# New times for the first eight chunks of x and for the first forgetting head in a one-core transformer block

## The chip, the cores and the metric

The kernel runs on one core of one Trainium2 chip. The metric is the device time of one execution in microseconds (us); lower is better. Engines are named as in the profile: PE (matrix products), DVE (vector), ACT (scalar and activations), POOL, and SP, which here issues nearly all DMA transfers. Each engine works through its own instructions strictly in program order and waits where an operand or a buffer is not ready.

## What is computed

One residual block on x of 512 x 2048 numbers in float32: a norm, one combined projection, eight stick-breaking heads and eight forgetting heads, an output projection, and an MLP.

```python
h = rmsnorm(x, g_attn[l])
proj = jnp.einsum('bsd,de->bse', h, w_in[l])
...
# forgetting heads, for each block i of 128 rows
z = jnp.einsum('bhqd,bhkd->bhqk', qb, kb).astype(jnp.float32) * scale
z = z + c[:, :, i * Q_BLOCK:end, None] - c[:, :, None, :end]
p = jax.nn.softmax(jnp.where(causal, z, -jnp.inf), axis=-1)
outs.append(jnp.einsum('bhqk,bhkd->bhqd', p.astype(v.dtype), vb))
...
mixed = jnp.concatenate([head_rmsnorm(o_sb, g_out_sb[l]),
                         head_rmsnorm(o_fox, g_out_fox[l])], axis=-1)
x = x + jnp.einsum('bse,ed->bsd', mixed, w_out[l])
h2 = rmsnorm(x, g_mlp[l])
u = jax.nn.relu(jnp.einsum('bsd,df->bsf', h2, w_up[l]))
x = x + jnp.einsum('bsf,fd->bsd', u * u, w_down[l])
```

## The kernel before

**Three products for one.** A float32 operand is split in a high part (a rounded cast, on ACT) and a low part (the operand less its high part, on DVE). A product is then three PE products: high by high, high by low, low by high. `mm3` issues the three (L76 to L78), which is why most PE rows carry these lines whatever they belong to. Weights follow the same way: a DMA to `wraw`, ACT's cast to `wh` (L168), DVE's rest `wl` (L171). The tile names `accq` (projections of the attention), `s` (scores), `w` (softmax weights), `pt` (their transposes), `ph` and `pl` (high and low part of these), `vh` and `vl` (of the values), `o` (a head's output) and `ssq` (its sum of squares) appear in the rows of the trace. `uh` and `ul` are high and low part of queries and keys, made from `qf`.

**The order is a table of times.** The program does not issue work directly. It collects jobs with `plan.at(t, f, ...)`, where t is a time on an imagined clock, and `plan.run()` calls them in the order of t. What counts is only the order that results: a job's time says behind and ahead of which others its instructions come on each engine. SP's transfers are issued by such jobs too. Nothing else arranges the engines' instructions.

**Stage 1, 0 to about 38 us.** x comes in 16 chunks of 128 columns, and the first value columns of the projection are summed over them in the order `seq` = 0, 1, 8, 9, 2, 10, 3, 11, 4, 12 and so on; `mm_at[j]` is the time of chunk j, 1.93 apart. For each chunk PE turns four blocks into the tile `tr` (`turn_x`, L256), of which there are two; ACT makes the high part (`x_high`, L259), DVE the low part (`x_low`, L262), and both tiles are also read for a scaled copy that the sums of the projection use later: `x_more` (DVE, L265) for the chunks below 8, `x_sum` (DVE, L271) and `x_right` (ACT, L268) for the others. The weights are `wfirst`. Chunks 0, 1, 8 and 9 are multiplied by kind: `first_part` (L299) does the four blocks of rows with high by high, then with high by low, then with low by high, and a table `early` gives each of their jobs a time. All others use `first_values`, which goes block by block with `mm3`, and share one list of times. `square_x` (ACT, L275) sums squares for the norm.

**Attention.** A period of `TPER` = 27.05 handles one head: its projections run in pieces between the steps of other heads. For a forgetting head, `plan_fox` places: `load` (a copy `cb` of the summed log forget gates), `start` (DVE adds them to the scores, L823; POOL masks, L768), `maxed` (DVE, L830 and L831), `soft` (ACT's exponentials with sums, L835), `scale` (DVE, L838 and L840). Then come `turn` (PE, ten transposes, L850), `p_high` (ACT, L859), `p_low` (DVE, L862), the twelve products of `o`, `square` (ACT, L889 to L891), `square_low` (DVE, L894) and `norm_sums` (PE, L899 and L900). The first head of all, number 0 in the order, is a forgetting one, and its steps lie between 184 and 216 us of the trace. `low_v` (L758) makes the low part of the values that it uses.

**Work beside it.** `WeightSums` forms sums of blocks of the output weights on DVE (L937, `mixed<-mixed` in the rows), with high and low parts on the way (`tboth`, L929 and L932; `thi`, L941 and L945) and stores to DRAM. `whole(m, t)` places them for m = 0 to 3. `scale_u`, `high_u` and `low_u` (L726 to L736) take queries and keys out of `accq`.

Of the kernel before, what the change touches and what calls it, by code (L numbers as in the profile page):

```python
# [19 lines left out]
NH = 8  # L20
# [16 lines left out]
def block_kernel(ctx, tc, x, g_attn, w_in, b_f, g_out_sb, g_out_fox, w_out, g_mlp, w_up, w_down, g_final, y):  # L37
# [101 lines left out]
    K8 = KC // 2  # L139
# [72 lines left out]
    with ExitStack() as stage:  # L212
# [23 lines left out]
        plan = Plan()  # L236
# [43 lines left out]
        c0, m = v_columns(order[0]), 2 * P + NH  # L280
# [25 lines left out]
        seq = [0, 1, K8, K8 + 1] + [j for k in range(2, K8) for j in (k, k + K8)]  # L306
# [36 lines left out]
        for j in seq[:4]:  # L343
            for part, wait in zip(("hh", "hl", "lh"), (0.0, 0.6, 1.1)):
                plan.at(mm_at[j] + wait, first_part, j, *pieces[j], part)
# [13 lines left out]
        for k in range(2, K8):  # L359
            t, j = mm_at[k], k + K8  # L360
            for jj, dt in ((k, 0.0), (j, step)):
                for half in range(2):
                    plan.at(t + dt + 0.74 * half, first_values, jj, *pieces[jj], half)
            w = pieces[k][0]
            cast, low = (-2.4, -1.4) if k == 2 else (-5.36, -3.91)
            jobs = [(-2.95, turn_x, k), (-2.2, x_high, k), (-1.5, x_low, k), (-0.75, x_more, k),
                    (-1.02, turn_x, j), (-0.3, x_high, j), (0.4, x_right, j), (0.85, x_low, j), (1.6, x_sum, j),
                    (cast, w.cast), (low, w.low)]
# [326 lines left out]
    with tc.tile_pool(name="att", bufs=1, side="right", reuse_waits="tile") as at, \  # L695
# [75 lines left out]
        class Head:  # L771
# [41 lines left out]
            def plan_fox(self, plan, t):  # L813
# [28 lines left out]
                for dt, f in ((-4.0, load), (10.85, start), (14.6, maxed), (16.8, soft), (20.1, scale)):  # L842
                    plan.at(t + dt, f)
# [108 lines left out]
        def whole(m, t):  # L952
# [8 lines left out]
            for dt, f in ((second[2] + 0.1, lambda: w.store(0, 2)), (TPER + (9.2 if m else 11.5), lambda: w.sum(2)), (TPER + (17.5 if m else 21.0), lambda: w.sum(3)),  # L961
                          (2 * TPER + 1.75, w.high_6), (2 * TPER + 2.5, w.low_6), (2 * TPER + 2.6, lambda: w.store(2, 4))):
                plan.at(t + dt, f)
# [43 lines left out]
        for n in range(2 * NH + 1):  # L1007
            t = TPER * n
            i_s, i_o = n - 1, n - 2
            if n < 2 * NH:  # L1010
# [18 lines left out]
                for which, dt in ((0, 21.4 if n else 19.0), (1, TPER + 0.3)):  # L1029
                    plan.at(t + dt, scale_u, n, which)  # L1030
                    plan.at(t + dt + 0.75, high_u, n, which)
                    plan.at(t + dt + 1.45, low_u, n, which)
# [16 lines left out]
            if 0 <= i_s < 2 * NH:  # L1049
# [4 lines left out]
                tp = t + 23.3 if n < 2 * NH else t + 2.9 + 1.95 + 1.45 * 11 - 0.05  # L1054
# [3 lines left out]
                if i_s % 2 == 0 and i_s < 2 * NH - 2:  # L1058
# [3 lines left out]
                    plan.at(t + (6.3 if i_s >= NH else 23.65), low_v, p_)  # L1062
# [23 lines left out]
        plan.at(52.0, free_loads)  # L1086
# [904 lines left out]
```

## Time and profile before

| | before |
|---|---|
| runs | 2033.85, 2033.62, 2033.54 us; median 2033.62 us |
| the profiled execution | 2033.73 us |
| its span, first to last instruction | 2032.0 us, so 1.7 us lie outside |
| mean granted PE clock | 0.998 |
| busy: PE / DVE / ACT / POOL | 2017.1 / 1739.4 / 1128.0 / 63.4 us |
| busy shares of the span | 99% / 86% / 56% / 3% |
| read from and written to HBM | 315.19 MB and 96.49 MB, 203 GB/s over the span |

A row of the timeline reads: start, duration, engine, line, operation, output<-inputs, partitions x elements, count. In brackets stands how long the engine sat idle just before, and what ended that. A matrix product's own duration overlaps the next one's, so the distance between two starts is what it costs. In a table of stretches, the granted clock stands behind the five engines' busy times, then the share of the DMA engines and GB/s. The waits view gives, for an engine and a line, what it waited for: us in total, times, longest.

### The profile page before, as it was taken

The numbers are of one execution on the slowest core, as the hardware profiler recorded it, in microseconds if no ns is written. First come the engines' busy times: TensorE is split into PE (matmuls) and PEld (weight loads), VectorE is DVE, ScalarE is ACT, GpSimd is POOL, SyncE is SP. The second block draws the span as 40 slices with busy tenths as digits, with TensorE's granted clock in tenths as the row PEclk, the third lists the DMA queues.
The fourth block names the chain that finished last, engine by engine and source line by source line (L and its number), as shares of the span: only waits on it lengthen the run. The fifth ranks groups of instructions, "written<-read, shape, count | busy, mean of one in ns | idle before, by whom it ended". The sixth has DMA issues, their size and how long they took to land.

```text
span 2032.0 us, 27211 instructions
## 1 busy us (share of the span) xinstructions
PE 2017.1 (99%) x10425; PEld 1745.0 (86%) x10425; DVE 1739.4 (86%) x1970; ACT 1128.0 (56%) x1619; POOL 63.4 (3%) x72
## 2 busy tenths in 40 slices
PE   9999999999999999999999999999999999999998
PEld 9998788888888889888888888888888888888886
DVE  7886777888877588899999999998799888888896
ACT  7544444555555556767767677676644343443444
POOL 0000101100000000000000000000000000000004
PEclk9999999999999999999999999999999999999999
DMA  7418566666548881666666666667685574674642
GB/s 246 166 66 261 182 196 194 200 202 202 181 128 283 293 275 60 225 191 190 210 205 185 213 202 200 204 196 253 247 301 199 223 260 168 235 254 175 220 163 83
DMA packets 270178, 413.45 MB, mean 203 GB/s; under 512 B 10280, under 2 KB 165976, under 8 KB 263520
## 3 DMA queue, kind: packets, MB, share of 16 engines
q1 hardware_dynamic: 269296, 409.61, 60.7%
q10 hardware_dynamic: 752, 2.11, 0.3%
q8 instruction: 82, 1.34, 0.3%
q14 instruction: 48, 0.39, 0.1%
HBM read 315.19 MB, written 96.49 MB: 203 GB/s over the span
## 4 chain that ended last, share of the span: by engine, by line
PE 93%; DVE 3%; DMA 1%; ACT 1%; issue 1%; POOL 0%; SPq 0%; ACTq 0%; POOLq 0%
PE psa L1224 10%; PE accd L78 8%; PE accd L76 8%; PE accd L77 8%; PE psa L1222 5%; PE accq L76 5%; PE accq L78 5%; PE accq L77 5%; PE psc L1224 5%; PE psc L1222 3%; PE psb L1224 3%; PE m L78 1%; PE m L77 1%; PE m L76 1%; PE psb L1222 1%; PE vy L78 1%
## 5 line engine op out<-in xcount | busy, mean ns | idle before, releaser
L1801 ACT CAST wh<-wd 128x1024 fp32r<-128x1024 f32 x126 | 124.9, 998 | 169.5 <-PE accd L78 54.6
L1691 DVE TENSOR_TENSOR wl<-wu,wh 128x1024 fp32r<-128x1024 f32 x158 | 192.6, 1220 | 13.0 <-ACT wh L1685 13.0
L76 PE MATMUL accq<-hH,wh 128*128 128x512 f32 x512 | 202.0, 395 | 0.0
L77 PE MATMUL accq<-hL,wh 128*128 128x512 f32 x512 | 200.1, 391 | 0.0
L78 PE MATMUL accq<-hH,wl 128*128 128x512 f32 x512 | 200.0, 391 | 0.0
L1685 ACT CAST wh<-wu 128x1024 fp32r<-128x1024 f32 x158 | 167.4, 1060 | 45.3 <-issue 22.7
L1224 PE MATMUL psa<-f,wh 128*128 128x512 f32 x720 | 179.0, 391 | 0.0
L77 PE MATMUL accd<-wl,uf 128*128 128x512 f32 x436 | 169.6, 389 | 0.0
L78 PE MATMUL accd<-wh,uf 128*128 128x512 f32 x436 | 169.6, 389 | 0.0
L76 PE MATMUL accd<-wh,uf 128*128 128x512 f32 x436 | 169.4, 389 | 0.0
L1224 PEld LDWEIGHTS psa<-f,wh 128*128 128x128 f32 x720 | 132.3, 188 | 25.6
L1808 DVE TENSOR_TENSOR wl<-wd,wh 128x1024 fp32r<-128x1024 f32 x126 | 144.0, 1152 | 10.6 <-ACT wh L1801 10.6
L1573 DVE TENSOR_TENSOR m<-m,accd 128x1024 f32<-128x1024 f32 x84 | 102.3, 1217 | 45.9 <-PE accd L78 45.9
L1801 ACT CAST wx<-wd 128x1024 fp32r<-128x1024 f32 (+1 forms) x82 | 80.8, 995 | 106.2 <-PE accd L78 39.8
L78 PEld LDWEIGHTS accq<-hH,wl 128*128 128x128 f32 x512 | 96.4, 188 | 20.4
L76 PEld LDWEIGHTS accq<-hH,wh 128*128 128x128 f32 x512 | 96.7, 189 | 18.6
L77 PEld LDWEIGHTS accq<-hL,wh 128*128 128x128 f32 x512 | 96.5, 189 | 18.7
L76 PE MATMUL accd<-wx,uf 128*128 128x512 f32 x284 | 110.5, 389 | 0.0
L77 PE MATMUL accd<-wx,uf 128*128 128x512 f32 x284 | 110.5, 389 | 0.0
L78 PE MATMUL accd<-wx,uf 128*128 128x512 f32 x284 | 110.5, 389 | 0.0
L168 ACT CAST wh<-wraw 128x1024 fp32r<-128x1024 f32 (+1 forms) x70 | 72.7, 1040 | 63.2 <-PE accq L77 51.3
L1222 PEld LDWEIGHTS psa<-f,wl 128*128 128x128 f32 x720 | 96.0, 191 | 5.9 <-ACT l L1255 0.6
(445 smaller groups left out, 5105.8 us busy)
## 6 DMA issues: line engine op xcount, KB each, us to landing
wu<-in_w_up_dram SPq DMA_DIRECT2D x60, 1024.0 KB, 6.6
ufd<-st SPq DMA_DIRECT2D x98, 512.0 KB, 3.8
wd<-in_w_down_dram SPq DMA_DIRECT2D x48, 1024.0 KB, 8.8
uf<-ufd SPq DMA_DIRECT2D x42, 1024.0 KB, 7.4
wraw<-in_w_in_dram SPq DMA_DIRECT2D x68, 512.0 KB, 4.4
wo<-wsums SPq DMA_DIRECT2D x28, 512.0 KB, 4.6
q<-in_w_in_dram SPq DMA_DIRECT2D x32, 384.0 KB, 6.2
wd<-in_w_down_dram SPq DMA_DIRECT2D x16, 768.0 KB, 6.5
```

The lines of the kernel that those rows point to most:

```text
L76: pe.matmul(out, sh, mh, start=first, stop=False, skip_group_check=True)
L77: pe.matmul(out, sh, ml, start=False, stop=False, skip_group_check=True)
L78: return pe.matmul(out, sl, mh, start=False, stop=last, skip_group_check=True)
L168: act.copy(self.hi, self.source())
L1222: ins = pe.matmul(ps[:, 2 * P:], lo[:, a, :], f_parts(p, a)[0], start=False, stop=last, skip_group_check=True)
L1224: ins = pe.matmul(ps, hi[:, a, :], f_both(p, a), start=a == PAIRS[0] and p in (1, 5), stop=last, skip_group_check=True)
L1573: dve.tensor_tensor(M[p][:, :, db, :], M[p][:, :, db, :], ps, op=ALU.add)
L1685: act.copy(rooms[k][0], srcs[k])
L1691: lows[0] = dve.tensor_tensor(lo, srcs.pop(k), hi.bitcast(F32), op=ALU.subtract)
L1801: act.copy(rooms[k + 3][0], srcs[k + 3])
L1808: dve.tensor_tensor(rooms[k + 2][1], srcs.pop(k + 2), rooms[k + 2][0].bitcast(F32), op=ALU.subtract)
```

## The change

Five things change, all of them times in the table:

- Chunks 2, 10, 3 and 11 join those that are multiplied by kind, and the table `early` holds new times for 0, 1, 8, 9 and these four. The loop over the other chunks begins at 4.
- Head 0's start, maxima, exponentials and scaling go to 6.5, 9.3, 11.0 and 14.0 of its period (from 10.85, 14.6, 16.8 and 20.1), its `turn` to 20.4 (from 23.3), with `p_high` and `p_low` behind it as before, and `low_v` of the first pair of heads to 17.0 (from 23.65).
- In `whole(0)` the third sum goes from `TPER` + 11.5 to `TPER` + 7.2 and the fourth from `TPER` + 21.0 to 2 `TPER` + 0.9.
- `scale_u` of the second head's first operand goes from 21.4 to 25.85.
- `free_loads`, which returns buffers, goes from 52.0 to 55.05.

```diff
-        for j in seq[:4]:
+        for j in seq[:8]:
             for part, wait in zip(("hh", "hl", "lh"), (0.0, 0.6, 1.1)):
                 plan.at(mm_at[j] + wait, first_part, j, *pieces[j], part)
...
         early = {0: ((-5.0, turn_x), (-4.1, "cast"), (-4.0, x_high), (-3.9, "low"), (-3.5, x_low), (-3.3, x_more)),
-                 1: ((-1.83, turn_x), (-1.8, "cast"), (-1.75, x_high), (-1.7, "low"), (-1.6, x_low), (-1.5, x_more)),
-                 8: ((-1.16, turn_x), (-1.1, "cast"), (-1.05, x_high), (-1.0, "low"), (-0.9, x_low), (-0.5, x_sum), (-0.4, x_right)),
-                 9: ((-2.59, turn_x), (-1.9, "cast"), (-1.85, x_high), (-1.6, x_right), (-1.5, "low"), (-1.4, x_low), (-1.3, x_sum))}
+                 1: ((-1.43, turn_x), (-1.8, "cast"), (-1.4, x_high), (-1.7, "low"), (-1.35, x_low), (-1.3, x_more)),
+                 8: ((-1.38, turn_x), (-1.19, "cast"), (-0.86, x_high), (-0.49, "low"), (-0.06, x_low), (0.69, x_sum), (1.21, x_right)),
+                 9: ((-2.81, turn_x), (-2.02, "cast"), (-1.59, x_high), (-0.79, "low"), (-0.36, x_low), (0.36, x_sum), (0.86, x_right)),
+                 2: ((-2.36, turn_x), (-2.22, "cast"), (-1.37, x_high), (-1.12, "low"), (-0.47, x_low), (0.28, x_more)),
+                 10: ((-2.36, turn_x), (-1.4, x_high), (-0.7, x_low), (0.05, x_sum), (0.55, x_right)),
+                 3: ((-2.36, turn_x), (-4.2, "cast"), (-1.9, x_high), (-1.43, "low"), (-0.73, x_low), (0.0, x_more)),
+                 11: ((-2.43, turn_x), (-2.03, x_high), (-1.53, x_right), (-1.08, x_low), (-0.33, x_sum))}
...
-        for k in range(2, K8):
+        for k in range(4, K8):
...
-                for dt, f in ((-4.0, load), (10.85, start), (14.6, maxed), (16.8, soft), (20.1, scale)):
+                times = (6.5, 9.3, 11.0, 14.0) if self.i == 0 else (10.85, 14.6, 16.8, 20.1)
+                for dt, f in zip((-4.0, *times), (load, start, maxed, soft, scale)):
                     plan.at(t + dt, f)
...
+            third, fourth = (TPER + 9.2, TPER + 17.5) if m else (TPER + 7.2, 2 * TPER + 0.9)
...
-                for which, dt in ((0, 21.4 if n else 19.0), (1, TPER + 0.3)):
+                for which, dt in ((0, {0: 19.0, 1: 25.85}.get(n, 21.4)), (1, TPER + 0.3)):
...
-                tp = t + 23.3 if n < 2 * NH else t + 2.9 + 1.95 + 1.45 * 11 - 0.05
+                tp = t + (20.4 if n == 1 else 23.3) if n < 2 * NH else t + 2.9 + 1.95 + 1.45 * 11 - 0.05
...
-                    plan.at(t + (6.3 if i_s >= NH else 23.65), low_v, p_)
+                    plan.at(t + (6.3 if i_s >= NH else 23.65 if p_ else 17.0), low_v, p_)
...
-        plan.at(52.0, free_loads)
+        plan.at(55.05, free_loads)
```

What this does to the order shows best at three places. The lines of the changed program are up to five higher for the same statement (L823 becomes L826, and so on).

ACT in stage 1, from the cast of chunk 8's weights on. Here `hH_97` and `hH_101` are the high parts of chunks below 8 and of the others, `x_132` is what `x_right` writes. Before:

```order
L168 COPY wh<-wfirst 128x264
L259 ACTIVATE hH_101<-tr,g_in 128x512
L268 ACTIVATE x_132<-tr,g_in 128x256
L168 COPY wh<-wfirst 128x264
L259 ACTIVATE hH_101<-tr,g_in 128x512
L268 ACTIVATE x_132<-tr,g_in 128x256
L168 COPY wh<-wfirst 128x528
L259 ACTIVATE hH_97<-tr,g_in 128x512
L168 COPY wh<-wfirst 128x528
```

And now:

```order
L168 COPY wh<-wfirst 128x264
L259 ACTIVATE hH_101<-tr,g_in 128x512
L168 COPY wh<-wfirst 128x264
L259 ACTIVATE hH_101<-tr,g_in 128x512
L268 ACTIVATE x_132<-tr,g_in 128x256
L168 COPY wh<-wfirst 128x528
L259 ACTIVATE hH_97<-tr,g_in 128x512
L268 ACTIVATE x_132<-tr,g_in 128x256
L168 COPY wh<-wfirst 128x528
```

`x_right` of chunks 8 and 9 moves behind the next chunk's cast and high part.

DVE around head 0, up to `pl`. Before, the start stood behind two sums, a low part of weights (`wl`) and `tboth`; these are the rows from the reciprocal on:

```order
L838 RECIPROCAL ml<-ml 128x4
L840 TENSOR_SCALAR w<-w,ml 128x128
L840 TENSOR_SCALAR w<-w,ml 128x256
L840 TENSOR_SCALAR w<-w,ml 128x384
L840 TENSOR_SCALAR w<-w,ml 128x512
L171 TENSOR_TENSOR wl<-wraw,wh 128x1024
L937 TENSOR_TENSOR mixed<-mixed 128x1024
L728 TENSOR_SCALAR qf<-accq,rb 128x512
L736 TENSOR_TENSOR ul<-qf,uh 128x512
L758 TENSOR_SCALAR vl<-vr,r1v,vh 128x256 x4
L862 TENSOR_TENSOR pl<-pt,ph 128x1280
```

Now, from the maxima on, with the low part of weights that has gone behind them:

```order
L833 TENSOR_REDUCE ml<-w 128x1 x4
L834 TENSOR_SCALAR ml<-ml 128x4
L171 TENSOR_TENSOR wl<-wraw,wh 128x1024
L936 TENSOR_TENSOR tboth<-mixed,tboth 128x512
L841 RECIPROCAL ml<-ml 128x4
L843 TENSOR_SCALAR w<-w,ml 128x128
L843 TENSOR_SCALAR w<-w,ml 128x256
L843 TENSOR_SCALAR w<-w,ml 128x384
L843 TENSOR_SCALAR w<-w,ml 128x512
L761 TENSOR_SCALAR vl<-vr,r1v,vh 128x256 x4
L171 TENSOR_TENSOR wl<-wraw,wh 128x1024
L866 TENSOR_TENSOR pl<-pt,ph 128x1280
```

Just ahead of these rows stand one `mixed<-mixed`, the four `w<-s,cq,cb` of the start and two more `mixed<-mixed`. Between the reciprocal and `pl` a sum, `qf` and `ul` are gone.

PE where head 0's output begins. Before, 13 projections lie between `pt` and `o`, and the products of `o` follow each other:

```order
L77 MATMUL accq<-hL_104,wh 128x512
L78 MATMUL accq<-hH_103,wl 128x512
L78 MATMUL accq<-hH_97,wl 128x512
L76 MATMUL o<-ph,vh 128x512
L77 MATMUL o<-pl,vh 128x512
L78 MATMUL o<-ph,vl 128x512
L76 MATMUL o<-ph,vh 128x384
```

And now:

```order
L78 MATMUL accq<-hH_97,wl 128x512
L76 MATMUL o<-ph,vh 128x512
L76 MATMUL accq<-hH_97,wh 128x512
L77 MATMUL accq<-hL_98,wh 128x512
L78 MATMUL accq<-hH_97,wl 128x512
L76 MATMUL accq<-hH_97,wh 128x512
L77 MATMUL o<-pl,vh 128x512
L78 MATMUL o<-ph,vl 128x512
```

`pt` has moved 14 matmuls ahead, 27 projections lie between it and `o`, four more between the first and the second product of `o`, and 11 between its last product and `ssq`, where there were 15.

More of the change, by code (lines that the diff above doesn't have):

```diff
@@ L960, in whole @@
                     plan.at(t + dt, f, i)
-            for dt, f in ((second[2] + 0.1, lambda: w.store(0, 2)), (TPER + (9.2 if m else 11.5), lambda: w.sum(2)), (TPER + (17.5 if m else 21.0), lambda: w.sum(3)),
+            third, fourth = (TPER + 9.2, TPER + 17.5) if m else (TPER + 7.2, 2 * TPER + 0.9)
+            for dt, f in ((second[2] + 0.1, lambda: w.store(0, 2)), (third, lambda: w.sum(2)), (fourth, lambda: w.sum(3)),
                           (2 * TPER + 1.75, w.high_6), (2 * TPER + 2.5, w.low_6), (2 * TPER + 2.6, lambda: w.store(2, 4))):
```

7 lines of the change are left out of this document (3 added, 4 removed).

## Prediction

> **What bounds the kernel now.** I read the waits of TensorE (PE) first, then the busy time by stages, then the rows of the two stretches in which PE is not full. The waits view lists only a handful of places in 2032 us:
>
> ```profile
> PE o L77 <- DVE pl L862: 2.1, 1, 2.1
> ...
> PE o L76 <- ACT ph L859: 0.6, 1, 0.6
> PE tr L256 <- DVE f L271: 0.5, 1, 0.5
> PE tr L256 <- ACT x L268: 0.4, 1, 0.4
> ```
>
> Each of these happens once (second number). The table of stretches (length, then PE, PEld, DVE, ACT, POOL busy, granted clock, DMA share, GB/s) says the same from the other side:
>
> ```profile
> 6.00:16.00 10.00, 8.92 (x70) 8.31 (x69) 7.50 (x14) 5.98 (x13) 0.00 (x0) 1.00 1.05 369
> 16.00:26.00 10.00, 10.00 (x84) 9.86 (x84) 8.56 (x15) 8.20 (x17) 0.00 (x0) 1.00 1.05 380
> 26.00:200.00 174.00, 173.96 (x982) 165.47 (x982) 134.76 (x163) 91.89 (x140) 2.33 (x5) 1.00 0.48 160
> 206.00:208.00 2.00, 0.51 (x1) 0.19 (x1) 2.00 (x5) 0.29 (x1) 0.00 (x0) 1.00 0.01 3
> 210.00:214.00 4.00, 4.00 (x16) 3.37 (x15) 2.38 (x4) 3.18 (x6) 0.00 (x0) 0.57 0.82 309
> 216.00:780.00 564.00, 564.00 (x2787) 478.65 (x2786) 435.19 (x558) 304.72 (x444) 39.77 (x46) 1.00 0.65 210
> ```
>
> PE sets the time: it is full from 16 us on, but for one hole at 206 us and a stretch behind it at little more than half the clock. So a gain can come from two places only: what is lost before 16 us, and what is lost around 206 us. The change reorders work at just these two. It adds and removes no instruction, so every price below is that of a wait, not of work.
>
> **Place 1: the first eight chunks.** The rows (start, duration) of the first product, the two delayed turnings, the first product by mm3, and two turnings of the full stretch with the product behind the second:
>
> ```profile
> 6.23 0.51 PE L299 MATMUL vy<-wh,hH 128*128 128x264 f32 x2
> ...
> 12.34 0.65 PE L256 MATMUL tr<-ident,xa 128*128 128x128 f32 x4 [0.44 <-ACT x L268]
> ...
> 14.98 0.63 PE L256 MATMUL tr<-ident,xa 128*128 128x128 f32 x4 [0.52 <-DVE f L271]
> ...
> 15.94 0.28 PE L76 MATMUL vy<-wh,hH 128*128 128x264 f32 x1
> ...
> 17.55 0.60 PE L256 MATMUL tr<-ident,xa 128*128 128x128 f32 x4
> ...
> 19.44 0.60 PE L256 MATMUL tr<-ident,xa 128*128 128x128 f32 x4
> 19.80 0.37 PE L76 MATMUL vy<-wh,hH 128*128 128x264 f32 x1
> ```
>
> The readers of the buffer that the turning at 12.34 needs, on DVE and ACT, and a later cast:
>
> ```profile
> 11.31 0.47 DVE L271 SCALAR_TENSOR_TENSOR f<-tr,g_in,x 128x256 f32<-128x256 f32 x1
> 11.81 0.47 ACT L268 ACTIVATE x<-tr,g_in 128x256 f32<-128x256 f32 x1 [1.21 <-DVE f L271]
> ...
> 18.77 0.62 ACT L168 CAST wh<-wfirst 128x528 fp32r<-128x528 f32 x1
> ```
>
> In the full stretch a chunk, twelve products and one turning, costs 19.44 - 17.55 = 1.89 us, and a turning puts off the next product by 19.80 - 19.44 = 0.36. Between 6.23 and 15.94 PE does four chunks and a fifth turning: 4 x 1.89 + 0.36 = 7.9 us of work in 9.7, so 1.8 lost. The cause is in the last rows: only two buffers hold turned chunks, ACT's and DVE's readers of one run one after the other (11.31, then 11.81), and the next turning waits for the last.
>
> The change gives each of eight chunks its own times, in the order in which its operands come, and multiplies chunks 2, 10, 3 and 11 by kind as well, so that PE has the high parts to work on while the low part is made. Walked through with the durations above, no turning waits up to chunk 11. There ACT's last reader of chunk 10 (0.47) stands behind a square, a high part and the cast of the fifth piece of weights; I estimate 0.4 us of wait left, so **1.4 of the 1.8 us are saved**. Bounds: 1.8 if that wait is nothing. Downwards: that cast ran at 18.77 before, and if its weights are not there sooner, the reader ends at 18.77 + 0.62 + 0.47 = 19.86, where I want the turning at some 17.5: 2.3 us lost, a loss of 0.5 in all.
>
> **Place 2: the first forgetting head.** PE's rows for it, and the first and last row of the same piece of the next head:
>
> ```profile
> 201.54 1.25 PE L850 MATMUL pt<-ident,w 128*128 128x128 f32 x10
> ...
> 204.70 0.39 PE L76 MATMUL accq<-hH,wh 128*128 128x512 f32 x1
> 204.93 0.39 PE L77 MATMUL accq<-hL,wh 128*128 128x512 f32 x1
> ...
> 206.35 0.51 PE L76 MATMUL o<-ph,vh 128*128 128x512 f32 x1 [0.58 <-ACT ph L859]
> ...
> 208.93 0.50 PE L77 MATMUL o<-pl,vh 128*128 128x512 f32 x1 [2.08 <-DVE pl L862]
> ...
> 215.77 0.40 PE L899 MATMUL ssq<-pl,onesr 128*128 128x512 f32 x1
> ...
> 233.12 1.25 PE L850 MATMUL pt<-ident,w 128*128 128x128 f32 x10
> ...
> 242.97 0.39 PE L899 MATMUL ssq<-pl,onesr 128*128 128x512 f32 x1
> ```
>
> The DVE rows between pt and the low part of pt, pl:
>
> ```profile
> 201.55 1.22 DVE L171 TENSOR_TENSOR wl<-wraw,wh 128x1024 fp32r<-128x1024 f32 x1
> 202.69 1.22 DVE L937 TENSOR_TENSOR mixed<-mixed 128x1024 f32<-128x1024 f32 x1
> 203.82 0.69 DVE L728 SCALAR_TENSOR_TENSOR qf<-accq,rb 128x512 f32<-128x512 f32 x1
> 205.20 0.69 DVE L736 TENSOR_TENSOR ul<-qf,uh 128x512 fp32r<-128x512 f32 x1 [0.69 <-ACT uh L732]
> 205.81 1.67 DVE L758 SCALAR_TENSOR_TENSOR vl<-vr,r1v,vh 128x256 fp32r<-128x256 f32 x4
> 207.39 1.48 DVE L862 TENSOR_TENSOR pl<-pt,ph 128x1280 fp32r<-128x1280 f32 x1
> ```
>
> The low part pl, which the second product of o needs, stands behind six other DVE jobs; PE has only 13 projections behind pt (order of PE), 204.93 - 204.70 = 0.23 us apart, and stands still for 0.58 and 2.08 us. The cost is more than these: head 0 takes 215.77 - 201.54 = 14.23 us from pt to ssq, the next head 242.97 - 233.12 = 9.85 with two projections more, so 9.85 - 0.46 = 9.4 is what head 0 should take. **4.8 us are lost**: 2.66 standing still, some 1.7 in the half clock (4 us at 0.57, of which 0.43 is lost) and about 0.5 in refilling. [...] Here the stretch at 0.57 stands right behind such a gap and nowhere else, so the trace decides for the gap as the cause.
>
> Now the changed order. It takes the sums, the first ul and one wl from between pt and pl and puts the low part of v ahead of pt; pt itself goes 14 matmuls earlier, to 201.54 - 14 x 0.23 = 198.3 on the old clock, and has 27 projections behind it before o begins (6.2 us instead of 3.0) and 4 more between o's first and second product (0.9).
>
> *Is pl in time?* DVE ends scaling w by 197.4 (below), then vl 1.67, wl 1.22: 200.3. ACT's high part (1.22) follows pt by 201. Then pl takes 1.48: 202.5. PE reaches the product that needs it at 198.3 + 1.0 + 6.2 + 0.2 + 0.9 = 206.6. Four us to spare.
>
> *Is w in time for the earlier pt?* This wait is new: pt now stands 3.2 us sooner, and PE runs in order, so all 27 projections are queued behind it. What starts the softmax was held up before by weights, as the chain of waits shows (start, length), and the next head gives the length of the steps from first w to last scaling:
>
> ```profile
> 179.59 9.33 DMA wraw<-in_w_in_dram
> 189.02 1.06 ACT wh L168
> 190.10 1.24 DVE wl L171
> ```
>
> DVE's rows of the sums, and the first and last step of the next head's softmax:
>
> ```profile
> 185.81 2.48 DVE L937 TENSOR_TENSOR mixed<-mixed 128x1024 f32<-128x1024 f32 x2
> ...
> 220.67 1.92 DVE L823 SCALAR_TENSOR_TENSOR w<-s,cq,cb 128x128 f32<-128x128 f32 x4
> ...
> 229.58 1.28 DVE L840 TENSOR_SCALAR w<-w,ml 128x128 f32<-128x128 f32 x4
> ```
>
> Head 0's w was queued on DVE behind a low part of weights whose transfer landed at 188.92. In the new order w stands ahead of that low part, right behind the first of the two sums that began at 185.81, so at 185.81 + 1.24 = 187.05. The next head needs 229.58 + 1.28 - 220.67 = 10.19 us, with two low parts of weights on DVE between where head 0 now has two sums (2.48): done by 197.4, with 0.9 us to spare before 198.3. Lower bound of the wait: none. Upper: w also needs cb, a copy issued just ahead of the 9.33 us transfer; were it to land as late as that one, 188.92, w would be 1.9 later and pt would wait 1.0.
>
> The low part of weights that now follows the maxima is done, by the walk, 3 to 4 us later than at 190.10 + 1.24. No row shows PE waiting for it before, and by PE's order its first user comes some 5 us after its new end: nothing, and at worst what is over 5. The later sums and ul have no reader before 212: nothing; their cover is the same projections. The square of o must now pass ACT and DVE within 11 projections before ssq, where the next head had 15 and waited for nothing (242.97): 0 to the four projections less, 0.9 us; I take 0, because ACT and DVE have nothing else to do there that is not also behind the next head's o. So **4.8 us are saved** at place 2; with the bounds on cb and the square 2.9 to 4.8.
>
> **The sum.** 1.4 + 4.8 = 6.2 us. From 216 us on PE is full and the order is as before; the loads are released by the work, so the shift should carry to the end. The profiled execution took 2033.73 us (span 2032.0 and 1.7 around it), 0.1 above the median 2033.62. 2033.73 - 6.2 = **2027.5 us**, 0.3% less; against the median the same to a tenth.
>
> **The rivals.**
>
> 1. *A short new wait for w, or place 1 returned.* For: the slack of 0.9 us comes from another head's rows, and the 9.33 us of the transfer beside cb say that the queues are full there, so cb and weights may not come 1.4 us earlier only because PE is. Against: the DMA share over 26 to 200 us is 0.48, so the queues fill late and from work that moves too. Price 1.0, or the 1.4 of place 1, or both: 2028.5 to 2029.9.
> 2. *The clock falls anyway.* If the half clock is not the gap's doing, the 1.7 stay: 2029.2. For: it sets in only once PE has run again for over a microsecond (208.93, and full clock up to 210). Against: PE is at 1.00 in the 174 us before and the 564 us behind, and three runs lie within 0.31 us, so nothing comes and goes. [...]
> 3. *The stall only moves.* PE waits for the earlier pt about as long as it waited for pl, 2 to 2.7 us, and the clock falls behind this gap as it did behind the other (1.7): only 0.6 to 1.1 of place 2 is left, and with place 1 some 2 us: 2031.5. For: pt is asked for 3.2 us sooner, and everything is queued behind it. Against: it would need w to be 3 to 3.6 us behind my walk.
> 4. *Slower: DVE stands still at w.* In its new place w is ahead of the weights' low part, the second and third sums and the maxima. If cb or the scores come late, all of these are late together and PE, waiting at pt, has nothing to do. PE stops once w is over 0.9 us late; with the clock's 1.7 the gain of 6.2 is used up at 0.9 + 4.5 = 5.4 us late, and 9.5 us late makes 2037.8, 0.2% slower. For: the transfer next to cb took 9.33 us. Against: cb is issued ahead of it and that one landed at 188.92, 1.9 after the time wanted.
>
> That the order does not change is excluded: the rows of DVE and PE stand differently at both places.
>
> **How the numbers follow.** Chances: forecast 0.57, rival 1 0.18, rival 2 0.05, rival 3 0.12, rival 4 0.08. About 0.2%, 4.1 us, is what a measurement of this kernel can tell from no change: faster than 2029.5 are the forecast, rival 2 and most of rival 1, **0.78**; the same are rival 3, the rest of rival 1 and a small part of rival 4, **0.15**; slower **0.07**. Predicted 2027.5. The range goes down to 2026.0 (place 1 whole, 0.4, and about 1 for refilling that my two rows of head 0 do not catch) and up to 2031.0, over rivals 1 and 2 and to the near edge of rival 3, leaving out about 0.2.
>
> **What would show it.** Place 1: the first mm3 product of chunk 4, eight chunks into the stage, comes 1.4 us sooner than before, PE in 6 to 16 us near 10 of 10. Place 2: o with no wait named behind it, a clock of 1.00 from 206 to 216 us, 9.4 to 9.6 us from pt to ssq. Wrong: a wait of pt for w or of tr for ACT's x, a granted clock under 1 anywhere from 180 to 220 us, or a span that shrinks less than the shift seen at 216 us.

## The result, and the profile after

| | before | changed |
|---|---|---|
| median of 22 runs each | 2032.09 us | 2028.72 us |
| lowest to highest | 2029.73 to 2034.01 us | 2027.99 to 2030.32 us |
| profiled execution, span | 2033.73, 2032.0 us | 2029.46, 2027.7 us |
| pt to ssq of head 0 | 14.23 us | 12.57 us, with 14 projections more in it |
| first product of the next stage | 38.96 us | 39.46 us |

The ratio is 0.9983 (95% interval 0.9977 to 0.9989): 3.4 us less, between 2.2 and 4.7. The forecast was 6.2 us less. The time lies in the range that was given, but little more than half of the gain came. The first three runs of the kernel before lay within 0.31 us; 22 runs span 4.3 us, those of the changed kernel 2.3. Nearly all that follows is about this spread. It also bears on the forecast itself, which started from 2033.73, 1.6 above the median of the 22 runs.

PE's waits in the changed kernel, from the view that showed four of interest before (us in total, times, longest):

```profile
PE vx L293 <- DVE still L289: 1.6, 1, 1.6
PE psa L78 <- DVE wl L59: 0.6, 2, 0.3
PE psa L1227 <- ACT l L1260: 0.4, 1, 0.4
PE tr L256 <- ACT x L268: 0.2, 1, 0.2
```

The waits of o for ph and pl are gone, and of those of tr 0.2 us are left. The first three were there before as well. The stretches that showed the hole:

```profile
6.00:16.00 10.00, 10.00 (x69) 9.72 (x69) 7.66 (x15) 5.74 (x12) 0.00 (x0) 1.00 1.06 375
16.00:26.00 10.00, 9.78 (x84) 9.57 (x82) 8.23 (x14) 8.66 (x17) 0.00 (x0) 1.00 1.02 367
...
206.00:208.00 2.00, 2.00 (x11) 1.69 (x10) 2.00 (x4) 1.14 (x2) 0.00 (x0) 1.00 0.91 276
210.00:214.00 4.00, 4.00 (x23) 3.49 (x22) 2.34 (x3) 3.01 (x5) 0.00 (x0) 1.00 0.66 237
```

PE is busy from 206 to 214 us, at a granted clock of 1.00 where 0.57 stood before. Head 0 on PE, in the timeline of the changed kernel:

```profile
198.88 1.25 PE L854 MATMUL pt<-ident,w 128*128 128x128 f32 x10
...
206.13 0.39 PE L76 MATMUL o<-ph,vh 128*128 128x512 f32 x1
...
207.26 0.39 PE L77 MATMUL o<-pl,vh 128*128 128x512 f32 x1
...
211.45 0.39 PE L903 MATMUL ssq<-pl,onesr 128*128 128x512 f32 x1
```

From pt to ssq it is 211.45 - 198.88 = 12.57 us. Less the 14 projections that pt now stands ahead of (14 x 0.227 = 3.18; in this stretch they start 0.227 us apart on the mean) this is 9.39, and the prediction wanted 9.4. Both of its slacks can be read on DVE:

```profile
186.85 1.93 DVE L826 SCALAR_TENSOR_TENSOR w<-s,cq,cb 128x128 f32<-128x128 f32 x4 [0.29 <-PE s L78]
...
195.76 1.27 DVE L843 TENSOR_SCALAR w<-w,ml 128x128 f32<-128x128 f32 x4
196.96 1.67 DVE L761 SCALAR_TENSOR_TENSOR vl<-vr,r1v,vh 128x256 fp32r<-128x256 f32 x4
198.54 1.22 DVE L171 TENSOR_TENSOR wl<-wraw,wh 128x1024 fp32r<-128x1024 f32 x1
201.44 1.49 DVE L866 TENSOR_TENSOR pl<-pt,ph 128x1280 fp32r<-128x1280 f32 x1 [1.68 <-ACT ph L863]
```

From the first w to the last scaling it is 195.76 + 1.27 - 186.85 = 10.18 us (10.19 was taken from the next head), done 1.85 us ahead of pt. pl is done at 202.93, 4.3 us ahead of the product that needs it.

So place 2 went as forecast in this profile: 4.8 us. Place 1 seems to have cost 0.5 us: 39.46 against 38.96. The rows say why:

```profile
9.28 0.64 PE L299 MATMUL vy<-wh,hL 128*128 128x264 f32 x2
9.72 0.63 PE L299 MATMUL vz<-wh,hL 128*128 128x264 f32 x2
10.16 0.43 PE L299 MATMUL vy<-wh,hH 128*128 128x264 f32 x2
10.43 0.41 PE L299 MATMUL vz<-wh,hH 128*128 128x264 f32 x2
10.68 0.60 PE L256 MATMUL tr<-ident,xa 128*128 128x128 f32 x4
```

Pairs of products start 0.44 us apart up to 10.16 and about 0.25 from then on: in this execution PE ran at half clock until 10.2 us. In the profile of the kernel before the full rate is there when the products begin (6.23, then 6.58 and so on, 0.24 for a pair soon after), and by the trace's clock record it came at 5.5 us. The granted clock reads 1.00 in both stretches, since the record begins with the first full clock; at the start the rate has to be read from the spacing of the rows. The two kernels run the same instructions up to the first product, so the change can't have moved this by itself. Two questions were left: what place 1 is worth at equal clock, and what place 2 is worth over many executions.

### The profile page after: what moved, and what is told of

The parts are those of the page before. It is cut to its first block, busy times and chain, and to the rows that moved or that the text cites. A ratio compares the mean times of both kernels' runs of the same rounds, so it can differ in the third digit from the quotient of the medians.

```text
span 2027.7 us, 27207 instructions
## 1 busy us (share of the span) xinstructions
PE 2016.1 (99%) x10425; PEld 1745.7 (86%) x10425; DVE 1739.6 (86%) x1970; ACT 1128.6 (56%) x1619; POOL 63.6 (3%) x72
## 3 DMA queue, kind: packets, MB, share of 16 engines
q10 hardware_dynamic: 752, 2.11, 0.3%
## 4 chain that ended last, share of the span: by engine, by line
PE 95%; DVE 3%; ACT 1%; issue 1%; DMA 0%; ACTq 0%
PE psa L1229 10%; PE accd L78 8%; PE accd L77 8%; PE accd L76 8%; PE accq L76 6%; PE accq L78 6%; PE accq L77 6%; PE psa L1227 5%; PE psc L1229 5%; PE psc L1227 3%; PE psb L1229 3%; PE m L77 1%; PE m L78 1%; PE m L76 1%; PE psb L1227 1%; PE vy L78 1%
## 5 line engine op out<-in xcount | busy, mean ns | idle before, releaser
L1813 DVE TENSOR_TENSOR wl<-wd,wh 128x1024 fp32r<-128x1024 f32 x126 | 144.0, 1151 | 10.6 <-ACT wh L1806 10.6
L78 PEld LDWEIGHTS accq<-hH,wl 128*128 128x128 f32 x512 | 96.1, 188 | 20.1
```

Of the source, the lines that this page charges most:

```text
L78: return pe.matmul(out, sl, mh, start=False, stop=last, skip_group_check=True)
L1813: dve.tensor_tensor(rooms[k + 2][1], srcs.pop(k + 2), rooms[k + 2][0].bitcast(F32), op=ALU.subtract)
```

## The experiments

The kernel before is timed beside each group of runs, on the same chip. All ratios are to it; they stand here as recorded, with their 95% intervals, and differ a little from the quotient of two medians. There were three groups, each on another chip, in which the kernel before had medians of 2033.94 us (one place at a time, the hole filled, idle products), 2033.37 (softmax, transposes put back, each kernel once more) and 2032.85 (the work beside it, transposes alone, both small repairs). The third profile of the kernel before is from a fourth chip.

**One place at a time.** In the first kernel only the first part of the diff (the table `early`, and chunks 2, 10, 3 and 11 by kind) is taken over, in the second all the rest of it.

> The kernel before with the new times of the first eight chunks alone; head 0 as before. Theory A (the reordering of stage 1 saves some 1.4 us when PE starts at full clock; in the profiled execution of the changed kernel it was hidden, because there the half clock at the start lasted to about 10.2 us instead of 5.5): end of stage 1 with a warm start near 37.5 us instead of 38.96, with a cold start near 39.5; against the kernel before, median 0.5 to 1.4 us faster. Rival B (the new order of stage 1 pays nothing and itself causes the late clock): 0 to 0.6 us slower, and a late clock in its profile. Head 0's waits of 0.6 and 2.1 us stay under both.

> The kernel before with the new times of head 0, of the sums of output weights, of the second head's first scaling and of the low part of v alone; stage 1 as before. Theory A: the waits at o are gone and pt to ssq is 9.4 us plus 0.23 for each projection that pt now stands ahead of; 2.7 to 4.8 us faster than the kernel before, depending on how often that kernel's clock really falls after its wait. Rival B: all of the 3.4 us measured for the whole change, neither more nor less, since stage 1 gives nothing.

The first part alone: 2032.11 us, ratio 0.9989 (0.9980 to 0.9998). The rest alone: 2029.27 us, 0.9979 (0.9971 to 0.9988). Both pay. The spread tells more: 2029.4 to 2033.8 for the first, where the hole at head 0 stays, and 2028.9 to 2030.0 for the second, where it is gone. In the profile of the first alone only one wait is left at o, and half clock follows it (granted clock 0.70 from 208 to 210 us, 0.50 from 210 to 212):

```profile
207.54 0.51 PE L77 MATMUL o<-pl,vh 128*128 128x512 f32 x1 [2.08 <-DVE pl L865]
```

**The hole filled, not removed.** In the kernel before, eleven idle products go to PE ahead of head 0's o.

```diff
 def product(self):
...
+    if self.i == 0:
+        for _ in range(11):
+            pe.matmul(self.o, onesr, hH[0], start=True, stop=True)
...
```

> The kernel before with eleven extra products of 512 columns (11 x 0.23 = 2.5 us) put on PE just ahead of head 0's o, into o's own buffer, which o's first product then overwrites: PE is busy in the hole of 2.66 us, and the wait for pl is no shorter. Theory A (the half clock behind the hole is caused by the hole, and costs 1.7 us where it comes): granted clock 1.00 from 206 to 216 us, up to 1.7 us faster than before, and the median 0.5 to 1.7 us faster. Rival (the half clock there has another cause): the clock falls all the same, and the time is the same or up to 0.3 us more.

2031.28 us, ratio 0.9990 (0.9981 to 0.9998), from 2030.6 to 2032.1 where the kernel before beside it spans 2030.5 to 2036.3. The stretches of its profile at the hole:

```profile
206.00:210.00 4.00, 3.95 (x18) 3.00 (x17) 3.71 (x7) 0.79 (x2) 0.00 (x0) 1.00 0.23 59
210.00:214.00 4.00, 4.00 (x23) 3.47 (x22) 2.51 (x4) 3.43 (x6) 0.00 (x0) 1.00 0.82 310
```

The clock stays at 1.00. PE did 2.5 us of work that nobody needs, and the kernel became faster for it and steadier. One profile alone would not show the hole as the cause of the half clock, since a profile of the kernel before without half clock follows below. The runs do: the longest of the eleven took 2032.14 us, and 22 of the 31 executions of the kernel before beside them took longer.

**Idle products at the start.** The changed kernel with seven in place of five ahead of the first product.

```diff
-plan.at(1.0, keep_busy, 5)
+plan.at(1.0, keep_busy, 7)
```

> The changed kernel with seven instead of five idle products ahead of the first product, so that PE has no gap between 6.2 and 6.5 us where it starts at half clock. [...] Rival (the lateness of the clock has nothing to do with that gap): the same median and spread as the changed kernel, within 0.3 us.

2028.86 us, 2028.3 to 2029.5, ratio 0.9973 (0.9963 to 0.9982). The changed kernel, timed on another chip, has 2028.87 and 2028.1 to 2029.8. The medians don't differ, and a spread of 1.2 against 1.7 us shows nothing. Whether the gap of 0.3 us matters to the clock stays open.

**Each kernel once more.** The kernel before was profiled twice more, the changed one once.

> The kernel before, unchanged, profiled once more. Theory (the clock is granted in windows of 3.41 us that run free of the program): the waits of 0.6 and 2.1 us at o stand as before, but the first full clock comes at another time than 5.5 us, anywhere from 5.4 to 10.3, and the half clock behind the hole comes at another time or not at all. Rival (the clock follows the program): full clock at 5.5 us and half clock from 210.3 us again, to within 0.3 us.

> The kernel before, unchanged, profiled a third time. Theory (free-running windows of 3.41 us): the waits at o stand again at 0.6 and 2.1 us; the half clock behind them lasts none, one or two windows, and pt to ssq takes 12.2, 14.2 or 15.7 us accordingly; the time goes with that and with the start: about 2031 with none, 2033 to 2034 with one, 2036 with two. Rival (something else in the kernel varies): a time that these two do not account for to within 1 us.

> The changed kernel, unchanged, timed beside the others on the same chip and profiled once more. Theory: the first full clock at another time than 10.2 us, and the end of stage 1 (first product of the next stage) between 38.0 and 39.5 us with it, 1.4 us sooner than the kernel before would have it with the same clock; 0.3 to 1 us faster than the version with the second place alone was against the kernel before. Rival (stage 1 pays nothing): end of stage 1 no sooner than 38.9 us.

The second profile of the kernel before took 2036.53 us, with three slices of half clock:

```profile
210.00:212.00 2.00, 2.00 (x6) 1.81 (x7) 1.31 (x3) 1.14 (x2) 0.00 (x0) 0.50 0.86 250
212.00:214.00 2.00, 2.00 (x9) 1.87 (x8) 0.48 (x1) 0.60 (x2) 0.00 (x0) 0.50 0.66 257
214.00:216.00 2.00, 2.00 (x6) 1.55 (x5) 0.97 (x2) 1.93 (x3) 0.00 (x0) 0.50 1.04 403
```

By the clock record the half clock lasted from 209.28 to 216.10, 6.82 us, twice the 3.41 of the first profile. The full clock at the start came at 7.9 us instead of 5.5. So the clock does not follow the program alone. The waits at o stand as they did:

```profile
207.36 0.49 PE L76 MATMUL o<-ph,vh 128*128 128x512 f32 x1 [0.69 <-ACT ph L859]
...
209.95 0.79 PE L77 MATMUL o<-pl,vh 128*128 128x512 f32 x1 [2.09 <-DVE pl L862]
```

The third took 2030.29 us and had no half clock there, but also another wait, which the theory had not foreseen:

```profile
207.17 0.50 PE L77 MATMUL o<-pl,vh 128*128 128x512 f32 x1 [1.17 <-DVE pl L862]
```

The hole was 1.17 instead of 2.66 us, with the same order on every engine. DVE's row of the start of head 0 in this third profile shows where that comes from, and behind it the cast that its queue waited for:

```profile
190.82 1.92 DVE L823 SCALAR_TENSOR_TENSOR w<-s,cq,cb 128x128 f32<-128x128 f32 x4
...
187.99 1.05 ACT L168 CAST wh<-wraw 128x1024 fp32r<-128x1024 f32 x1 [4.02 <-DMA wraw<-in_w_in_dram]
```

In the first profile this w started at 192.59, its cast at 189.02 and the cast of tboth at 191.33; here 190.82, 187.99 and 189.31. In the second profile w started at 193.60. So the whole chain up to pl hangs on transfers, and these land one to two us sooner or later from one execution to the next. That these profiles are not all from one chip is not the reason: on one chip alone, 31 executions of the kernel before span 5.9 us. Three profiles of one program give 15.73, 14.23 and 10.83 us from pt to ssq, or 6.3, 4.8 and 1.4 us more than the 9.4 that head 0 needs. The five profiles with the changed order of head 0 (the changed kernel twice, the second place alone, the two with seven idle products) have 12.56 to 12.58. The executions that were timed without a profile go the same way: of the 31 beside the first group, the five with a mean granted clock of 0.997 took 2035.7 to 2036.3 us, the 12 with 0.999 took 2030.5 to 2034.3, and the 14 with 0.998 lie anywhere from 2030.7 to 2036.2 (the mean also counts the end, where PE has no work).

The changed kernel took 2028.87 us in this group, 2028.1 to 2029.8, ratio 0.9981 (0.9973 to 0.9990). In its second profile w had to wait, and the scaling ended later than in the first:

```profile
188.06 1.93 DVE L826 SCALAR_TENSOR_TENSOR w<-s,cq,cb 128x128 f32<-128x128 f32 x4 [0.52 <-DMA cb<-ckd]
...
196.99 1.28 DVE L843 TENSOR_SCALAR w<-w,ml 128x128 f32<-128x128 f32 x4
```

That is 198.27, where pt began at 198.14 with the blocks that were scaled first; it shows no wait, but nothing is left of the 1.85 us. The margin at pt, too, depends on when a transfer lands.

This profile has full clock from 8.0 us by the record, and ends stage 1 at 38.75. With all profiles the value of place 1 can be read at equal clock (full clock from, by the clock record; first product of the next stage, from the timeline):

| old order of stage 1 | | new order of stage 1 | |
|---|---|---|---|
| third profile of before | 5.4, 38.98 | changed, with both small repairs (below) | 5.0, 37.70 |
| first profile of before | 5.5, 38.96 | changed, transposes put back (below) | 5.9, 37.66 |
| hole filled | 7.7, 39.60 | changed, softmax put back (below) | 6.2, 37.64 |
| second profile of before | 7.9, 39.72 | changed, work beside it put back (below) | 6.5, 37.75 |
| second place alone | 8.2, 39.92 | changed, seven idle products | 6.8, 38.09 |
| | | first place alone | 7.4, 38.16 |
| | | changed, second profile | 8.0, 38.75 |
| | | changed, first profile | 10.2, 39.46 |
| | | first place and transposes alone (below) | 10.6, 39.71 |

At 5 to 6 us the new order is 1.3 us ahead, at 8 us 1.0 to 1.1. Within the columns the end of the stage moves with the clock by 1 us on the left and 2 us on the right.

**What in place 2 does it.** Three versions put single parts of it back, a fourth has a single part alone.

The first puts head 0's softmax back:

```diff
-times = (6.5, 9.3, 11.0, 14.0) if self.i == 0 else (10.85, 14.6, 16.8, 20.1)
+times = (10.85, 14.6, 16.8, 20.1) if self.i == 0 else (10.85, 14.6, 16.8, 20.1)
```

> The changed kernel with head 0's start, maxima, exponentials and scaling back at their old times, the earlier transposes and all else kept. It prices rival 4 of the prediction. Theory (pt is only free of a wait because the softmax is earlier too): w is scaled at about 201.5 us less the shift of stage 1, pt is due 3.2 us sooner, so PE waits at pt for DVE's scaling for about 3 us, and in some executions the half clock of 3.41 us follows: 3 to 5 us slower than the changed kernel, about the time of the kernel before. Rival (the slack in the trace is larger than the walk says): no wait of pt over 1 us and less than 1 us slower than the changed kernel.

2029.59 us, ratio 0.9986 (0.9977 to 0.9995). The theory missed: pt waited 0.2 us, not 3.

```profile
197.36 1.97 PE L854 MATMUL pt<-ident,w 128*128 128x128 f32 x10 [0.18 <-DVE w L843]
```

The transposes then followed the scaling block by block and took 1.97 us instead of 1.25, so that pt to ssq is 13.28 us where the changed kernel has 12.56: 0.7 us lost in all, and the clock did not fall. The scaling ended at 198.29 where I had put it at about 200, for two reasons. From the first w to the last scaling it took 8.55 us instead of 9.04, since with the sums moved DVE's queue had one job of 1.22 us less ahead of the maxima. And w started at 189.74, some 1.5 us sooner than the 192.59 of the first profile of before less the shift of stage 1, because the transfers that DVE's queue stands behind landed sooner (the casts behind them started at 186.91 and 188.25, where 189.02 and 191.33 stood): this part is a draw. But none of the eleven runs is above 2030.6 us, and the median is 0.7 us above the changed kernel's in the same group. The earlier softmax is a margin, not the source of the gain.

The second puts the transposes back:

```diff
-tp = t + (20.4 if n == 1 else 23.3) if n < 2 * NH else t + 2.9 + 1.95 + 1.45 * 11 - 0.05
+tp = t + (23.3 if n == 1 else 23.3) if n < 2 * NH else t + 2.9 + 1.95 + 1.45 * 11 - 0.05
```

> The changed kernel with head 0's transposes and the two parts of them back at the old time (12 projections later than now), all else kept, so that DVE's order is that of the change and only PE's is moved back in part: 15 projections lie between pt and o instead of 27. Theory (what held o back before was DVE's jobs ahead of pl, and 5.8 us of cover up to the product that needs pl are enough for the 3.95 us of pt, ph and pl): no wait at o, same as the changed kernel within 0.3 us. Rival (the earlier transposes carry the gain): a wait of 0.5 to 2 us at o and as much in the time.

2031.59 us, ratio 0.9992 (0.9983 to 1.0001), from 2030.1 to 2033.0, and 2.7 us above the changed kernel in the same group. The theory missed. The waits at o are gone, but ssq now waits:

```profile
211.43 0.51 PE L903 MATMUL ssq<-pl,onesr 128*128 128x512 f32 x1 [1.74 <-ACT pl L895]
...
212.16 0.50 PE L904 MATMUL ssq<-pl,onesr 128*128 128x512 f32 x1 [0.22 <-DVE pl L898]
```

I had counted the cover up to o and not beyond. The granted clock stayed at 1.00. In PE's order of this version 25 projections stand between pt and o (not 15), 5 between o's first two products, and none between o and ssq, where the changed kernel has 11. The projections of the stretch are one store for all of head 0's waits: what is used up ahead of o is missing behind it, and an earlier pt makes the store larger.

The third puts back the work beside it (and with the second head's scaling its `high_u` and `low_u`, which the change also has 0.1 sooner behind that scaling):

```diff
-third, fourth = (TPER + 9.2, TPER + 17.5) if m else (TPER + 7.2, 2 * TPER + 0.9)
+third, fourth = (TPER + 9.2, TPER + 17.5) if m else (TPER + 11.5, TPER + 21.0)
...
-for which, dt in ((0, {0: 19.0, 1: 25.85}.get(n, 21.4)), (1, TPER + 0.3)):
+for which, dt in ((0, 21.4 if n else 19.0), (1, TPER + 0.3)):
     plan.at(t + dt, scale_u, n, which)
-    plan.at(t + dt + (0.65 if (n, which) == (1, 0) else 0.75), high_u, n, which)
-    plan.at(t + dt + (1.35 if (n, which) == (1, 0) else 1.45), low_u, n, which)
+    plan.at(t + dt + 0.75, high_u, n, which)
+    plan.at(t + dt + 1.45, low_u, n, which)
...
-plan.at(t + (6.3 if i_s >= NH else 23.65 if p_ else 17.0), low_v, p_)
+plan.at(t + (6.3 if i_s >= NH else 23.65), low_v, p_)
```

> The changed kernel with both sums of the output weights, the low part of v and the second head's first scaling back at their old times; head 0's softmax and transposes stay at the new ones. DVE then has a low part of weights, a sum, qf and ul ahead of pl again, about 1.6 us more than in the changed kernel. Theory (pl has some four us to spare, so what stands ahead of it does not matter once pt is earlier): no wait at o over 0.3 us and within 0.5 us of the changed kernel, with its small spread. Rival (it is DVE's queue ahead of pl that the change mends): a wait of 1 to 2 us at o and as much in the time.

2029.30 us, ratio 0.9984 (0.9975 to 0.9992). No wait at o, though DVE's queue ahead of pl is nearly that of before:

```profile
210.42 0.50 PE L903 MATMUL ssq<-pl,onesr 128*128 128x512 f32 x1 [0.54 <-ACT pl L895]
...
211.15 0.50 PE L904 MATMUL ssq<-pl,onesr 128*128 128x512 f32 x1 [0.23 <-DVE pl L898]
```

The 0.5 us are again at ssq, ahead of which 5 projections are left instead of 11, 10 standing between o's first two products. So DVE's order ahead of pl matters little once pt is earlier; with the 0.8 us at ssq it is not quite nothing.

The fourth is the kernel with the first place alone, and of the second only the transposes:

```diff
-tp = t + 23.3 if n < 2 * NH else t + 2.9 + 1.95 + 1.45 * 11 - 0.05
+tp = t + (20.4 if n == 1 else 23.3) if n < 2 * NH else t + 2.9 + 1.95 + 1.45 * 11 - 0.05
```

> The kernel with the new stage 1 alone, and of the second place only the earlier transposes of head 0; its softmax, the sums, the low part of v and the second head's scaling stay at their old times. Theory (the earlier transposes need an earlier softmax, by either its own times or the sums being out of its way): w is scaled at about 200.7 us, pt is due 3 us before that, so PE waits at pt for DVE's scaling for 2.5 to 3.3 us, no wait at o remains, and no, one or two stretches of half clock of 3.41 us follow: 2 to 5 us slower than the changed kernel, with a spread over the runs of 3 us or more. Rival (as the version with the softmax alone put back showed, the old softmax is early enough): wait of pt under 1 us, within 1 us of the changed kernel.

2031.84 us, ratio 0.9993 (0.9984 to 1.0002), from 2028.1 to 2032.6. The wait has moved to pt, and nothing is left at o:

```profile
201.44 1.97 PE L853 MATMUL pt<-ident,w 128*128 128x128 f32 x10 [1.75 <-DVE w L843]
```

This is the wait of rival 3 of the prediction, seen on the chip, but without the clock's fall. Its w started at 193.32, again behind a cast that waited. The transposes are again drawn out to 1.97 us. The wait of 1.75 us was not followed by half clock in this profile. Three of its eleven runs are as fast as the changed kernel (2028.1 to 2029.2); that these are the ones in which the transfers land soon is likely, but none was profiled.

**A version with both small repairs.** Seven idle products, and ACT's last reader of chunk 10 ahead of the cast:

```diff
-10: (..., (0.05, x_sum), (0.55, x_right)),
+10: (..., (0.05, x_sum), (0.38, x_right)),
```

> The changed kernel with seven idle products at the start instead of five, and ACT's last reader of chunk 10 ahead of the cast of the fifth piece of weights. Theory: the 0.2 us wait of the turning of chunk 11 for ACT is gone; 0.2 us less than the changed kernel, which is under what its runs can tell. Rival (the cast, 0.5 us later, is now waited for): a wait of PE for weights in 20 to 24 us.

2028.52 us, ratio 0.9981 (0.9971 to 0.9990), against 0.9981 and 0.9983 for the changed kernel: no difference that can be told. The wait for ACT is gone, but the same turning still has 0.3 us of idle time ahead of it in the waits, with nothing named that it waited for. Ten runs lie between 2027.9 and 2029.7. An eleventh took 4104 us; it is left out of the ratio, there is no profile of it, and its cause is not known.

## Why the prediction was right, and where not

- *Place 1, 1.4 us.* The mechanism held: the turnings no longer wait but for 0.2 us (0.4 was left over in the sum, though such a wait was also named as a sign of being wrong), and at equal clock the stage ends 1.0 to 1.3 us sooner. What the prediction did not have is that the time of the first full clock is not a property of the kernel (5.5, 7.9 and 5.4 us in the three profiles of the kernel before). The profile it was made from had full clock at 5.5 us, nearly the earliest of all; the changed kernel's first profile had it at 10.2, which hid the gain altogether.
- *Place 2, pl in time, w in time.* Both walks were right to some tenths: 10.18 us for the softmax, 4.3 us of slack at pl, no wait at ssq. The slack at pt, put at 0.9, was 1.85 in one profile and nothing in the other, where w waited 0.52 us for cb; the upper bound had named this wait, and pt still did not have to.
- *The sum.* This is the step that failed in size: "4.8 us are saved", taken as what the kernel before always loses. It is what it lost in one execution. The three profiles lost 1.4, 4.8 and 6.3. Two things differ from execution to execution: when the weights and sums land that DVE's queue stands behind, and whether the half clock after the hole lasts no, one or two stretches of 3.41 us (by the reading in the last section, after the hole's length and how it lies to the clock's steps). With the hole only filled, pt to ssq took 12.23 us, so one stretch costs 14.23 - 12.23 = 2.0 and two cost 15.73 - 12.23 = 3.5, PE's restart included. The medians contain the cheap executions too, hence 3.4 us where 6.2 were forecast. With 1.0 to 1.3 for place 1 and 0.5 lost again at the very end (below), 2.6 to 2.9 us are left for place 2 in those 22 runs; in the first group of experiments the second place alone gave 4.3 by its ratio and 4.7 by the medians.
- *The time.* That 2028.7 came nearer to the forecast 2027.5 than the gain to its 6.2 is luck: the profile from which it was reckoned, and the first three runs, lay 1.5 to 1.6 us above the median of the 22. Reckoned from that median, the same sum would have given 2025.9, 2.8 us off.
- *"Three runs lie within 0.31 us, so nothing comes and goes"*, said against rival 2, was wrong. Rival 2 itself (the half clock is not the hole's doing) fell with the filled hole. The clock term was right in cause and wrong as a constant.
- *Slips in the working.* The rows show five DVE jobs between pt and pl, not six. 187.05 + 10.19 is 197.2, not 197.4. Rival 3 at its worst leaves 4.8 - 2.7 - 1.7 = 0.4 of place 2, not 0.6. None of them moves the forecast.
- *Rivals 3 and 4* priced a wait for w at pt. It appears if the transposes alone are moved; the sums' new places or the new softmax times were each enough, in the profiles and runs made, to prevent most of it.
- *The shift carries.* From ssq to the end it is 1816.2 us before, 1816.3 after, and 1815.1 to 1817.2 over all the profiles. Most of this goes either way, but the last part does not. From the start of the last product to the end it takes 8.57 or 8.58 us in the three profiles of the kernel before and the one with the hole filled, 9.03 to 9.10 in the four that have the whole change, and 8.29 to 8.36 in the six with parts of it. The last store of the result is issued 3.9 us behind that product in all of them, and lands 3.3 us later, or 4.0 in the four with the whole change. That store is the longest in this view of the stores to `out_dram`, first of the kernel before, then of the changed one:

```profile
DMA to landing us min/median/max: 2.5/2.7/3.3
...
DMA to landing us min/median/max: 2.5/2.7/4.0
```

The prediction had no such term: some 0.5 us of the gain are lost here. Against the versions with parts of the change it is 0.7 to 0.8, and that fits with the second place alone (2029.27) and the changed kernel with seven idle products (2028.86), timed in one group, lying only 0.4 apart. Why this store lands later is not known.

- One sentence of the kernel's description is too strong: that nothing but the table arranges the engines. Four projections stand between the first two products of o though one job issues all twelve, and with other times for DVE's jobs alone it was ten. What moves them was not traced.

## What to carry to other kernels

Where a wait ends on a chain that begins with a transfer, its length in one profile is one draw; a second and third profile of the same kernel would have given 1.4 to 6.3 us here instead of 4.8. A change that takes the wait off such a chain can buy a narrow spread (here 2.3 instead of 4.3 us) besides a lower median. When PE's steps are moved, count the work that covers every later step that waits, not only the next: here ssq was out of cover as soon as o had it all.

## What the runs showed of the hardware that was not expected

In three profiles a hole of 2 us or more on PE was followed by half clock: for 3.41 us with waits of 0.58 and 2.08 (the first profile of the kernel before) and of 2.08 alone (the first place alone), for 6.82 us with 0.69 and 2.09 (the second of the kernel before). The granted clock stayed at 1.00 behind waits of 1.17 (the third of the kernel before), of 1.75 (the transposes alone), and of 1.74 and 0.22 (the transposes put back).

What the falls have in common can be read from the clock record. In the three profiles with half clock at head 0 the fall comes 204.80, 201.39 and 201.39 us after the first full clock, which is 60, 59 and 59 times 3.4133. So in these profiles the clock changes on a grid of 3.413 us, and this grid lies differently in each of them: the first full clock came at 5.48 in the first profile of the kernel before, at 7.89 in the second, at 7.41 with the first place alone. Laid out on the grid, the step of 3.413 us just ahead of the fall holds 2.07, 2.11 and 2.08 us in which PE is idle by the profile. In the profiles without a fall the waits give no step more than 1.75 us (the transposes alone); the 1.74 and 0.22 of the transposes put back are split by the grid into 1.06 and 0.90. The end of the kernel, where PE runs out of work, says the same in all fourteen profiles: steps with 2.08 us of idle time and more are followed by half clock (2.46 in the first profile of the kernel before), and steps with 1.70 and 1.71 are not (1.70 in the first of the changed kernel). In these profiles the bound thus lies between 1.75 and 2.07 us out of 3.413. That the same hole would cost something or nothing by how it lies is an estimate from this; no two profiles here show it. The second step of half clock, in the second profile of the kernel before, follows a step that still holds 0.67 us of the wait; in the other two that step holds none of it.

At the start full clock came anywhere from 5.0 to 10.6 us in the fourteen profiles, with the same instructions on PE up to the first product but for the idle ones added. The end of stage 1 moves with it by 1 to 2 us. The range of 5.6 us is longer than one step of 3.413, so where the grid lies can account for only part of it; on which step full clock comes differs too, and the record does not show why.
